# Column sums of the modulation vectors: two rows on two 32-column quarters of TensorE

## The chip, the cores and the metric

The kernel runs on one core of a Trainium2 chip. The core has a matrix engine (TensorE; in the profile PE for the matmuls and PEld for the weight loads), a vector engine (VectorE, DVE), a scalar engine (ScalarE, ACT), a general engine (GpSimd, POOL) and a queue engine (SyncE, SP), which in this kernel issues the DMAs. Matmuls read SBUF and write PSUM. The metric is the device time of one execution in microseconds.

## The reference

One step of a hybrid diffusion backbone with one layer: 128 context tokens and 2048 latent tokens, 1024 wide. What the change touches is the modulation: six vectors of 1024 for each of two conditionings (context and latent), from one matrix product.

```python
def modulation(cond, w_mod_l, b_mod_l):
    m = jax.nn.silu(cond) @ w_mod_l + b_mod_l
    return jnp.split(m[:, None, :], N_MOD, axis=-1)
...
def block(x, s0, mod, n_chunks, ...):
    sh1, sc1, ga1, sh2, sc2, ga2 = mod
    h = rmsnorm(x, norm_mix_l) * (1.0 + sc1) + sh1
    o, s_new = mixer(h, s0, n_chunks, ...)
    x = x + ga1 * o
    h = rmsnorm(x, norm_ffn_l) * (1.0 + sc2) + sh2
    x = x + ga2 * (jnp.square(jax.nn.relu(h @ w_ff1_l)) @ w_ff2_l)
    return x, s_new
```

The mixer holds two DeltaNet scans and a spatial gate between one input and one output projection.

## The kernel before

The kernel runs in stages. Up to about 400 us it normalises the tokens, projects them (`pj`, lines 220 to 222 with operands `kH`, `kL`, `wH`, `wL`), convolves (`cv`) and stores queries, keys and values. Then come the scans with the other projections and the output projection (to about 1238 us), and then the two FFN products, whose matmuls write the PSUM tile `f`. Nearly every matmul is one of three of `mm3` (lines 220 to 222): both operands are split into a high and a low part that are read as fp32r, and high x high, high x low and low x high are added up in PSUM. ScalarE makes the high parts and VectorE the low ones.

The 6144 columns of the modulation product are worked off in twelve chunks `jc` of 512. Chunks 0 to 3 come first, by plain matmuls (line 335). Chunk 4 is done by `split_mod_steps`. The other seven, 5 to 9 in the first stage and 10 and 11 in the first FFN product, are made by `mod_steps`. There a chunk's eight blocks of 128 x 512 weights are loaded one after the other (line 235), and VectorE multiplies each by a column of the activated conditioning `scond` and adds it up (lines 254 and 256) into two accumulators `acc`, one for each conditioning, of 128 partitions x 512. What is left is a sum over the 128 partitions, made by TensorE in `total()`: one fp32 matmul for each accumulator (line 270) with the weights `pick[:, c, :]`, two columns wide, of which column c holds ones and the other zeros. Both matmuls add into the same two PSUM partitions. VectorE then adds the bias row (line 274), which `bias` (line 265) has loaded onto two partitions, and a DMA stores both rows to `mod_d` in DRAM (line 275).

In the first stage the steps of a chunk are given out beside the feature tiles by `interleave`, and the row tile `mrow` has one buffer. In the FFN the steps are spread over the products from the middle on, the accumulators and the row are `macc` tiles, and `total` is a step of its own (`pair` is given there). The readers of `mod_d` are the column step `second_mods` (line 718, chunks 6 to 9), the rows of the first gate (line 213, chunks 4 and 5) and those of the second (line 1853, chunks 10 and 11).

What order the instructions of an engine have is settled when the program is built: the calls and their written-out times give a first order, and the tile framework places instructions by a simulated timeline (`_TC = dict(schedule_with_timeline_sim=True)`). All DMAs are issued by SP, in one order.

Of the kernel before, what the change touches and what calls it, by code (L numbers as in the profile page):

```python
# [8 lines left out]
F32 = mybir.dt.float32  # L9
# [5 lines left out]
ALU = mybir.AluOpType  # L15
# [3 lines left out]
P = 128  # L19
# [43 lines left out]
def hybrid_step(  # L63
# [7 lines left out]
    V, A, G, T = nc.vector, nc.scalar, nc.gpsimd, nc.tensor  # L71
    load = nc.sync.dma_start
    store = nc.sync.dma_start
# [18 lines left out]
    mod_d = dp.tile([2, 6 * D], F32, name="mod_d")  # L92
# [73 lines left out]
    smp = ctx.enter_context(tc.tile_pool(name="small", bufs=4, reuse_waits="tile"))  # L166
# [40 lines left out]
    def w512(name, dt=F32):  # L207
        return wp.tile([P, 512], dt, tag="w", name=name)
# [12 lines left out]
            T.matmul(ps, lh, rl, start=False, stop=False, skip_group_check=more)  # L221
            T.matmul(ps, ll, rh, start=False, stop=last and i == n - 1, skip_group_check=more)  # L222

    pick = smp.tile([P, 2, 2], F32, tag="pick", name="pick", bufs=1)
    V.memset(pick, 0.0)
    V.memset(pick[:, 0, 0:1], 1.0)
    V.memset(pick[:, 1, 1:2], 1.0)

    def mod_steps(jc, pool, stage=None, psum=None, pair=None):

        u = {}

        def fetch_raw(k):
            raw = stage() if stage else sp.tile([P, 512], F32, tag="raw", name="raw")
            load(out=raw, in_=w_mod[0, k * P : (k + 1) * P, jc * 512 : (jc + 1) * 512])
            return raw

        def f(k):
            if pair:
                if k == 0:  # L240
                    u[0], u[1] = fetch_raw(0), fetch_raw(1)
                raw = u.pop(k)
                if k + 2 < KT:
                    u[k + 2] = fetch_raw(k + 2)
            else:
                raw = fetch_raw(k)
            if k == 0:
                if pair:
                    u["acc"] = pair()
                else:  # L250
                    u["acc"] = [pool.tile([P, 512], F32, tag=f"acc{c}", name="acc", bufs=1) for c in range(2)]
            for c, acc in enumerate(u["acc"]):
                if k == 0:
                    V.tensor_scalar_mul(acc, raw, scond[:, k, c : c + 1])
                else:
                    V.scalar_tensor_tensor(out=acc, in0=raw, scalar=scond[:, k, c : c + 1], in1=acc,
                                           op0=ALU.mult, op1=ALU.add)
            if k == KT - 1 and not pair:
                total()
            elif k == KT - 1:  # L260
                u["row"] = pair()[0][0:2, :]
                bias(u["row"])

        def bias(row):
            load(out=row, in_=b_mod[0:1, jc * 512 : (jc + 1) * 512].to_broadcast([2, 512]))

        def total():
            ps = (psum or pm1)()
            for c, acc in enumerate(u["acc"]):
                T.matmul(ps[0:2, :], pick[:, c, :], acc, start=c == 0, stop=c == 1)  # L270
            row = u["row"] if pair else pool.tile([2, 512], F32, tag="mrow", name="mrow", bufs=1)
            if not pair:
                bias(row)
            V.tensor_tensor(out=row, in0=ps[0:2, :], in1=row, op=ALU.add)
            store(out=mod_d[:, jc * 512 : (jc + 1) * 512], in_=row)

        return [lambda k=k: f(k) for k in range(KT)] + ([total] if pair else [])

    head = {}

    with ExitStack() as ph:
# [8 lines left out]
        def pt():  # L290
            return ppt.tile([P, 512], F32, tag="pt", name="pt", bufs=3)
# [93 lines left out]
        ps = pt()  # L385
# [328 lines left out]
        def second_mods():  # L714
# [8 lines left out]
            for cd in range(2):  # L723
                V.scalar_tensor_tensor(out=a2[:, cd, :], in0=pc4[:, cd, 1, :], scalar=1.0, in1=vec[:, 24:32],
                                       op0=ALU.add, op1=ALU.mult)

        mods = [st for jc in range(4, 10) for st in (split_mod_steps(jc) if jc == 4 else mod_steps(jc, p1))]
        blk, xs_, cols = prep_block(0)
        for st in xs_:
# [30 lines left out]
        for bi in range(len(BLOCKS)):  # L760
# [8 lines left out]
            for n, (gi, h) in enumerate(order):  # L769
                u = us[n] if bi == 0 and n < 3 else feature_tile(blk, bi, gi, h)  # L770
# [156 lines left out]
    with ExitStack() as ph:  # L927
# [551 lines left out]
        for i, u in enumerate(units):  # L1479
# [3 lines left out]
            c = i % 2  # L1483
# [107 lines left out]
    def bank():  # L1591
        return psq.tile([P, 512], F32, tag="f", name="f", bufs=8)
# [19 lines left out]
    class Unit:  # L1612
# [6 lines left out]
        def load(self, i, kh):  # L1619
            for q in range(2):  # L1620
                self.raw[i, kh, q] = r = w512("raw")
                r0, c0 = kh * 512 + q * 256, self.jp * 512 + i * 256
                load(out=r.rearrange("p (a c) -> p a c", a=2),
                     in_=w_ff1[0, r0 : r0 + 256, c0 : c0 + 256].rearrange("(a p) c -> p a c", p=P))
# [130 lines left out]
    acc = {}  # L1755
# [210 lines left out]

    junk16 = smp.tile([P, 512], BF16, tag="junk16", name="junk16", bufs=1)
    mods = [st for jc in range(10, 12) for st in mod_steps(jc, wp, lambda: w512("mraw"), bank, mrow)]
    mods = {half + 28 + 4 * j: st for j, st in enumerate(mods)}

# [8 lines left out]
    for p, (o, n, m) in enumerate(seq):  # L1979
        u = units[n]  # L1980
# [37 lines left out]
    for m, (n, i, u, q) in enumerate(todo):  # L2018
# [6 lines left out]
        if q == 0:  # L2025
            ps = bank()
# [80 lines left out]
```

## Time and profile before

| what | us |
|---|---|
| median of 3 runs | 2574.07 |
| lowest and highest of the runs | 2570.79, 2575.09 |
| the profiled execution's own time | 2574.06 |
| its span in the profile | 2572.3 |
| PE busy | 2536.5 |
| PEld busy | 2132.5 |
| DVE busy | 1782.1 |
| ACT busy | 1192.8 |
| POOL busy | 315.1 |

The span is the time from the first to the last recorded instruction; the execution's own time has 1.8 us around it. The mean granted TensorE clock was 0.999. Busy times of different engines lie beside each other. A weight load usually lies beneath the matmul before it, so PEld and PE do not add up. A recorded matmul includes the end of its pipeline, so the pace is read from one start to the next. In a view of groups a row gives the line, the engine, the operation, the output and inputs and the count, then the least, median and greatest duration in ns and the first and last start in us. In a view of waits a row gives who waited, for whom, the total in us, the number of times and the longest.

### The profile page before, as it was taken

Reading aid. Unit: us, or ns where it says so; the run is one execution under the profiler, and the core shown is the slowest. Engines: PE = TensorE matmul, PEld = TensorE weight load, DVE = VectorE, ACT = ScalarE, POOL = GpSimd, SP = SyncE. Lnnn points to the kernel's source line nnn. Section 1 sums busy time; section 2 is a strip of 40 time slices with the busy share of each in tenths; the row PEclk is TensorE's granted clock in tenths of the full one; section 3 lists DMA queues with packets and bytes.
Section 4 is the critical chain, followed back from the end, with each engine's and each line's share of the span. In section 5 each row is a group of like instructions: output and inputs, shape, how many; then the busy total and the mean of one; then the engine's idle time right before and its main releaser. Section 6 shows DMA issues by size and latency. Waiting matters only on the chain.

```text
span 2572.3 us, 43717 instructions
## 1 busy us (share of the span) xinstructions
PE 2536.5 (99%) x15296; PEld 2132.5 (83%) x15296; DVE 1782.1 (69%) x3525; ACT 1192.8 (46%) x2758; POOL 315.1 (12%) x512
## 2 busy tenths in 40 slices
PE   8999999999999999999999999999999999999998
PEld 4999999788888788778888888888888888888887
DVE  5777746667667788885587886677674445684874
ACT  4755545554545566763355553333243333243441
POOL 3112112222222233331000000000000000000000
PEclk9999999999999999999999999999999999999999
DMA  8966637755556758896778788445599778686773
GB/s 285 299 225 205 191 126 219 246 161 171 171 169 179 228 185 270 279 304 209 274 219 249 221 289 279 140 147 152 180 299 323 267 258 296 241 259 211 232 253 105
DMA packets 533859, 579.77 MB, mean 225 GB/s; under 512 B 35500, under 2 KB 366684, under 8 KB 530054
## 3 DMA queue, kind: packets, MB, share of 16 engines
q1 hardware_dynamic: 533638, 576.98, 69.3%
q8 instruction: 120, 1.97, 0.3%
q14 instruction: 101, 0.83, 0.1%
HBM read 397.62 MB, written 179.22 MB: 224 GB/s over the span
## 4 chain that ended last, share of the span: by engine, by line
PE 55%; DVE 1%; issue 1%; DMA 0%; ACT 0%; POOL 0%; DVEq 0%; POOLq 0%; ACTq 0%
PE f L220 17%; PE f L221 17%; PE f L222 17%; PE pj L220 1%; PE pj L222 1%; PE pj L221 1%; PE f L856 0%; PE pd L994 0%; PE pd L1098 0%; PE pd L1099 0%; DMA hop_d<-opL 0%; PE pm L1415 0%; PE pd L1062 0%; PE f L270 0%; PE f L1738 0%
## 5 line engine op out<-in xcount | busy, mean ns | idle before, releaser
L220 PE MATMUL f<-hop,zH 128*128 128x512 f32 x960 | 373.2, 389 | 0.0
L222 PE MATMUL f<-hop,zL 128*128 128x512 f32 x960 | 373.1, 389 | 0.0
L221 PE MATMUL f<-hop,zH 128*128 128x512 f32 x960 | 373.1, 389 | 0.0
L220 PE MATMUL f<-hop,wH 128*128 128x512 f32 x896 | 351.4, 393 | 0.0
L221 PE MATMUL f<-hop,wH 128*128 128x512 f32 x896 | 348.9, 390 | 0.0
L222 PE MATMUL f<-hop,wL 128*128 128x512 f32 x896 | 344.3, 390 | 0.0
L1601 ACT CAST zH<-zraw 128x512 fp32r<-128x512 f32 x240 | 146.3, 620 | 286.1 <-DVE zraw L1595 87.4
L1595 DVE TENSOR_TENSOR zL<-zraw,zH 128x512 fp32r<-128x512 f32 x240 | 162.2, 687 | 77.6 <-ACT zH L1601 66.1
L221 PEld LDWEIGHTS f<-hop,zH 128*128 128x128 f32 x960 | 180.2, 188 | 37.4
L222 PEld LDWEIGHTS f<-hop,zL 128*128 128x128 f32 x960 | 180.2, 188 | 37.4
L220 PEld LDWEIGHTS f<-hop,zH 128*128 128x128 f32 x960 | 180.2, 188 | 37.3
L222 PEld LDWEIGHTS f<-hop,wL 128*128 128x128 f32 x896 | 168.2, 188 | 35.7
L220 PEld LDWEIGHTS f<-hop,wH 128*128 128x128 f32 x896 | 168.5, 188 | 33.9 <-issue 0.9
L221 PEld LDWEIGHTS f<-hop,wH 128*128 128x128 f32 x896 | 168.5, 188 | 32.2
L222 PE MATMUL pj<-kH,wL 128*128 128x386 f32 (+2 forms) x568 | 190.5, 335 | 0.0
L220 PE MATMUL pj<-kH,wH 128*128 128x386 f32 (+2 forms) x568 | 189.2, 336 | 0.5 <-DVE kH L487 0.3
L221 PE MATMUL pj<-kL,wH 128*128 128x386 f32 (+2 forms) x568 | 189.3, 333 | 0.0
L178 POOL TENSOR_TENSOR r<-rsq,nhalf 128x1 f32<-128x1 f32 (+1 forms) x38 | 23.0, 605 | 1351.8 <-DVE rsq L177 1351.8
L1748 ACT CAST wH<-s 128x512 fp32r<-128x512 f32 x96 | 58.9, 620 | 172.5 <-DVE s L1595 156.9
L537 DVE SCALAR_TENSOR_TENSOR cv<-pj,vec,cv 128x384 f32<-128x384 f32 (+2 forms) x164 | 87.1, 539 | 56.9 <-ACT cv L534 55.5
L220 PEld LDWEIGHTS pj<-kH,wH 128*128 128x128 f32 x568 | 107.1, 189 | 5.1 <-issue 4.7
L221 PEld LDWEIGHTS pj<-kL,wH 128*128 128x128 f32 x568 | 107.4, 189 | 0.5
(409 smaller groups left out, 5726.5 us busy)
## 6 DMA issues: line engine op xcount, KB each, us to landing
zraw<-z_d SPq DMA_DIRECT2D x212, 256.0 KB
raw<-in_w_ff_dram SPq DMA_DIRECT2D x128, 256.0 KB
hop<-hop_d SPq DMA_DIRECT2D x28, 1024.0 KB
z_d<-c SPq DMA_DIRECT2D x96, 256.0 KB
zraw<-s_d SPq DMA_DIRECT2D x96, 256.0 KB
raw<-in_w_mod_dram SPq DMA_DIRECT2D x80, 256.0 KB
r<-in_w_ff_dram SPq DMA_DIRECT2D x80, 256.0 KB
s_d<-s SPq DMA_DIRECT2D x64, 256.0 KB
```

The lines of the kernel that those rows point to most:

```text
L178: G.tensor_tensor(out=out, in0=t[:np_, :n], in1=nhalf[:np_, :n], op=ALU.pow)
L220: T.matmul(ps, lh, rh, start=first and i == 0, stop=False, skip_group_check=more)
L221: T.matmul(ps, lh, rl, start=False, stop=False, skip_group_check=more)
L222: T.matmul(ps, ll, rh, start=False, stop=last and i == n - 1, skip_group_check=more)
L537: V.scalar_tensor_tensor(out=cv[:, o : o + m], in0=ps[:, s + sh : s + sh + m], scalar=convw[:, w, j : j + 1], in1=cv[:, o : o + m], op0=AL ...
L1595: V.tensor_tensor(out=out, in0=a, in1=b, op=op)
L1601: A.copy(h, src)
L1748: A.copy(h, s2)
```

## The change

The two accumulators are no longer summed into two neighbouring partitions by matmuls of two columns each. `pick` is now one block of 32 columns with ones in the first and zeros in the others (a tile of 40 columns is allocated, of which 32 are used). Each accumulator has its own matmul, the first with its output on PSUM partitions 0 to 31, the second on 32 to 63, each started and stopped by itself. The sums stand on partitions 0 and 32. So the row tile reaches to partition 32, and the bias load, the add and the store are done once for each of the two rows.

```diff
-    pick = smp.tile([P, 2, 2], F32, tag="pick", name="pick", bufs=1)
+    pick = smp.tile([P, 40], F32, tag="pick", name="pick", bufs=1)[:, 0:32]
     V.memset(pick, 0.0)
-    V.memset(pick[:, 0, 0:1], 1.0)
-    V.memset(pick[:, 1, 1:2], 1.0)
+    V.memset(pick[:, 0:1], 1.0)
...
             elif k == KT - 1:
-                u["row"] = pair()[0][0:2, :]
+                u["row"] = pair()[0][0:33, :]
                 bias(u["row"])
 
+        def one(c):
+            return slice(32 * c, 32 * c + 1)
+
         def bias(row):
-            load(out=row, in_=b_mod[0:1, jc * 512 : (jc + 1) * 512].to_broadcast([2, 512]))
+            for c in range(2):
+                load(out=row[one(c), :], in_=b_mod[0:1, jc * 512 : (jc + 1) * 512])
 
         def total():
             ps = (psum or pm1)()
             for c, acc in enumerate(u["acc"]):
-                T.matmul(ps[0:2, :], pick[:, c, :], acc, start=c == 0, stop=c == 1)
-            row = u["row"] if pair else pool.tile([2, 512], F32, tag="mrow", name="mrow", bufs=1)
+                T.matmul(ps[32 * c : 32 * c + 32, :], pick, acc, start=True, stop=True)
+            row = u["row"] if pair else pool.tile([33, 512], F32, tag="mrow", name="mrow", bufs=1)
             if not pair:
                 bias(row)
-            V.tensor_tensor(out=row, in0=ps[0:2, :], in1=row, op=ALU.add)
-            store(out=mod_d[:, jc * 512 : (jc + 1) * 512], in_=row)
+            for c in range(2):
+                V.tensor_tensor(out=row[one(c), :], in0=ps[one(c), :], in1=row[one(c), :], op=ALU.add)
+                store(out=mod_d[c : c + 1, jc * 512 : (jc + 1) * 512], in_=row[one(c), :])
```

## The prediction, made before the change was run

> **What bounds the kernel now.** I began with the head of the profile page: which engine fills the span, and what the chain that ended last consists of.
>
> ```profile
> span 2572.3 us, 43717 instructions
> PE 2536.5 (99%) x15296; PEld 2132.5 (83%) x15296; DVE 1782.1 (69%) x3525; ACT 1192.8 (46%) x2758; POOL 315.1 (12%) x512
> PE 55%; DVE 1%; issue 1%; DMA 0%; ACT 0%; POOL 0%; DVEq 0%; POOLq 0%; ACTq 0%
> ```
>
> TensorE is busy for 99% of the span and is the only engine with weight in the chain; busy matmul time alone can mislead, because matmuls overlap. So I next read the busy time by stretches, in those parts where the change has its work (five of its seven places lie between 150 and 350 us, two between 1700 and 1850 us) and in what follows. The columns are the stretch, its length, and the busy time and count of PE, PEld, DVE, ACT and POOL.
>
> ```profile
> 150.00:200.00 50.00, 50.00 (x308) 47.58 (x307) 33.99 (x63) 25.75 (x73) 7.67 (x33) 1.00 0.73 242
> 300.00:350.00 50.00, 50.00 (x297) 45.83 (x296) 36.10 (x72) 26.98 (x80) 11.45 (x36) 1.00 0.57 179
> 400.00:650.00 250.00, 244.88 (x1990) 205.04 (x1989) 167.04 (x435) 127.59 (x312) 57.98 (x55) 1.00 0.66 206
> 650.00:900.00 250.00, 246.15 (x2192) 204.86 (x2188) 182.78 (x471) 132.34 (x289) 62.20 (x70) 1.00 0.60 185
> 900.00:1238.00 338.00, 329.87 (x2793) 274.60 (x2792) 265.95 (x581) 199.19 (x531) 98.38 (x87) 1.00 0.75 240
> 1700.00:1850.00 150.00, 150.00 (x735) 124.16 (x734) 104.03 (x165) 52.15 (x94) 0.00 (x0) 1.00 0.52 158
> ```
>
> The reader is to see that PE has no idle time at all where the changed matmuls stand (50.00 of 50, 150.00 of 150), at granted clock 1.00, and that DVE has 14 to 16 us free in every 50 there and 46 in the 150. PE is idle only between 400 and 1238 us: 5.12 + 3.85 + 8.13 = 17.1 us. Thus a microsecond of PE time saved at the seven places comes off the end, and work added to DVE or to the DMA queue there costs nothing until it makes PE wait.
>
> **The matmuls that change.** The rows of the tile `pick` come next, then the weight loads around one of the seven places.
>
> ```profile
> L270 PEld LDWEIGHTS pm<-acc,pick x20: 80/84/85, 153.8 to 348.7; 128*2 128x2 f32 x20
> L270 PE MATMUL pm<-acc,pick x20: 591/592/593, 153.8 to 349.1; 128*2 128x512 f32 x20
> L270 PE MATMUL f<-macc,pick x8: 591/592/592, 1719.0 to 1823.6; 128*2 128x512 f32 x8
> ```
>
> ```profile
> 153.38 0.34 PE L221 MATMUL pj<-kL,wH 128*128 128x386 f32 x1
> 153.56 0.33 PE L222 MATMUL pj<-kH,wL 128*128 128x386 f32 x1
> 153.83 1.88 PE L270 MATMUL pm<-acc,pick 128*2 128x512 f32 x4
> 155.64 0.44 PE L220 MATMUL pj<-kH,wH 128*128 128x386 f32 x1
> ```
>
> ```profile
> 153.83 0.09 PEld L270 LDWEIGHTS pm<-acc,pick 128*2 128x2 f32 x2 [0.25 <-issue]
> 154.26 0.08 PEld L270 LDWEIGHTS pm<-acc,pick 128*2 128x2 f32 x1 [0.35 <-issue]
> 154.69 0.09 PEld L270 LDWEIGHTS pm<-acc,pick 128*2 128x2 f32 x1 [0.34 <-issue]
> 155.63 0.19 PEld L220 LDWEIGHTS pj<-kH,wH 128*128 128x128 f32 x1 [0.86 <-issue]
> ```
>
> The counts are 20 and 8 where the source has two matmuls at each of 5 and 2 places: each fp32 matmul runs as two passes, with a weight load each, so one place has four passes (x4). The loads stand at 153.83 (two), 154.26 and 154.69; a load for the next pass goes out as the running pass begins, so a pass takes 154.26 - 153.83 = 154.69 - 154.26 = 0.43 us. The recorded 592 ns is longer than that because the ends overlap. From the first pass to the next ordinary matmul it is 155.64 - 153.83 = 1.81 us, which is 4 x 0.43 = 1.72 and 0.09 at the way out; at the way in, 153.83 - 153.56 = 0.27 against 0.18 for neighbours (153.56 - 153.38), another 0.09. The seven places together hold 7 x 4 x 0.43 = 12.0 us of passes, 0.47% of the span. That is all that can be won here.
>
> **The change part by part.** *Two column quarters.* Each row gets a matmul of its own (32 columns of weights, of which the first holds ones), the first into PSUM partitions 0 to 31, the second into 32 to 63. The number of passes stays four. What can change is that passes on different columns of the array run side by side. Passes go out in program order: first row pass 1, first row pass 2, second row pass 1, second row pass 2. Pass 2 of a row needs the same columns as its pass 1 and cannot start beside it; pass 1 of the second row can start right behind pass 2 of the first. That makes three slots of 0.43 in place of four: pass 1, then two together, then the last. No row of this trace shows two column parts in use at once, so the gain is bounded from both sides: no overlap gives 0, both rows wholly side by side saves two slots, 0.86 a place or 6.0 us. I take one slot, 7 x 0.43 = 3.0 us, because the row of loads shows that passes start in order and that a load is the only thing that goes out ahead.
>
> *Wider weights.* The row for a load of 128 columns is this:
>
> ```profile
> L221 PEld LDWEIGHTS f<-hop,zH 128*128 128x128 f32 x960 | 180.2, 188 | 37.4
> ```
>
> A load of 2 columns takes 84 ns and one of 128 columns 188 ns, so one of 32 columns should take about 84 + 30 x 104 / 126 = 109 ns, 25 more.
>
> Loads go out beneath the pass before, except the first of a place: 7 x 0.025 = +0.2 us. Bounds: 0 if the way in hides it, and +0.7 us if 25 ns are paid on all four loads (28 x 0.025). I take 0.2. The ways in and out (0.09 each) remain, since the matmuls of 2 columns already stand apart from full ones.
>
> Here a rule speaks against the change. The loads at 154.26 and 154.69 go out while a pass with all 128 rows is running. The Trainium skill, "TensorE: Matmul & The Clock Gate", section "Part 3: Packing small matmuls — row/col tiling", says that a weight load overlaps a running matmul only where the row groups differ; two column quarters share all four row groups, and by that rule the second row's load would wait and no slot be won. This trace disagrees for loads into the same columns; no row shows it for other columns.
>
> *Two adds and two bias loads in place of one.* The add on two partitions and the two DMAs are these:
>
> ```profile
> L274 DVE TENSOR_TENSOR mrow<-pm,mrow x5: 669/673/679, 156.5 to 349.7; 2x512 f32<-2x512 f32 x5
> L275 SPq DMA_DIRECT2D mod_d<-mrow x5: 248/253/319, 157.2 to 350.4; - x5
> L265 SPq DMA_DIRECT2D mrow<-in_b_mod_dram x5: 261/262/273, 127.3 to 306.6; - x5
> ...
> L1595 DVE TENSOR_TENSOR acc<-f,acc x18: 678/692/692, 2194.0 to 2481.1; 128x512 f32<-128x512 f32 x18
> ...
> DVE cv L537 <- ACT cv L534: 50.9, 27, 5.2
> SPq L275 <- DVE mrow L274: 6.2, 4, 2.4
> SPq L265 <- DMA mod_d<-mrow: 2.1, 3, 1.3
> PE pj L220 <- DVE cv L537: 0.2, 1, 0.2
> PE pj L609 <- DVE cv L537: 0.2, 1, 0.2
> ...
> ACT junk L435 <- DMA x<-in_x_sample_dram: 17.7, 6, 5.4
> ```
>
> The add of 2 partitions takes 0.67 us and one of 128 partitions 0.69, so one partition should cost as much as two: seven more adds, 7 x 0.67 = 4.7 us of DVE time. DVE spends 50.9 us between 120 and 415 us waiting for ACT's `cv`, so the 3.4 us that fall there fit in; PE waits for DVE 0.4 us in all of that time (the two PE rows). If that cover were gone each add would put `cv` or a weight split 0.67 us later, 4.7 us at most; I take 0. The queue gets 14 more DMAs: 7 x (0.25 + 0.26) = 3.6 us of issue. Behind the waiting instructions on SP stand the raw loads for later modulation steps, the stores of `kH`, `kL` and the features, and the x loads. SP already stands 6.2 us before its stores for the add and 2.1 us before the next bias load for the store (`mrow` has one buffer); each second store waits 0.67 more, and the next bias load for two stores. Who waits for what SP brings is ACT at the x loads (17.7 us in that time), not PE. Cost 0; bound, as above, the whole 3.6. The other reader is the column step at L718:
>
> ```profile
> L718 SPq DMA_DIRECT2D mrow<-mod_d x1: 767/767/767, 351.6 to 351.6; - x1
> L720 PE MATMUL pt<-ident,mrow x1: 243/243/243, 414.9 to 414.9; 32*128 32x32 f32 x1
> ...
> L1853 SPq DMA_DIRECT2D row<-mod_d x4: 320/320/320, 2369.4 to 2458.1; - x4
> L275 SPq DMA_DIRECT2D mod_d<-macc x2: 249/252/254, 1721.6 to 1825.5; - x2
> ```
>
> It loads at 351.6 and its transpose runs at 414.9, 63 us later; a second store behind it by under 2 us changes nothing. What the last two places write by 1825.5 us is read from 2369.4 us on.
>
> *The ones.* The memsets of `pick` look like this:
>
> ```profile
> L226 DVE MEMSET pick<- x1: 59/59/59, 1.7 to 1.7; 128x1 f32 x1
> ```
>
> Three of them become two; they end at 1.7 us, 152 us ahead of their first reader. I take 0. `pick` takes 160 bytes a partition in place of 16, so tiles placed behind it move.
>
> ```profile
> L222 PE MATMUL f<-hop,zL 128*128 128x512 f32 x960 | 373.1, 389 | 0.0
> L220 PE MATMUL f<-hop,wH 128*128 128x512 f32 x896 | 351.4, 393 | 0.0
> ```
>
> The FFN matmuls read operands from dozens of buffers, and the means of their groups lie between 389 and 393 ns. So I take 0 for the places; one nanosecond on each of these 5568 matmuls, either way, would be 5.6 us.
>
> **The sum.** -3.0 + 0.2 = -2.8 us against the profiled execution's 2574.06 us, which is 0.01 us from the median of the three runs (2574.07): **2571.2 us**, 0.11% less.
>
> **The rivals.** *No overlap* (the change doesn't do what it says): the second quarter's load or pass waits for the first. For it: nothing in the trace has ever run side by side. Against it: loads do go out ahead. Time: 2574.06 + 0.2 to 0.7, say 2574.5.
> *Both rows wholly side by side*: passes of the two rows pair up, two slots a place. For it speaks only that they share nothing but the order; against it, the order. Time: 2574.06 - 6.0 + 0.2 = 2568.2. The Trainium skill, in the section named above, gives packed matmuls a span of one matmul and about 4 ns for each further part, which amounts to this case; no row here shows it.
> *Slower, a new order*. Two of the longest waits of PE are these:
>
> ```profile
> PE pd L1189 <- DVE P L1178: 4.8, 10, 1.4
> PE pj L1415 <- DVE o L1400: 3.8, 3, 1.3
> ```
>
> The program is ordered at build time by a simulated timeline (`schedule_with_timeline_sim=True`). Longer adds and more DMAs there can shift what stands where between 400 and 1238 us, where PE already idles 17.1 us, about half of it at these two handovers. If that idle time grew by half, 8.5 us, the time would be 2574.06 - 2.8 + 8.5 = 2579.8. It makes the kernel slower than before from 2.8 us of growth on. Against it: the edits lie outside this stretch, 50 us before it or 480 after it, and between 350 and 400 us PE is full again.
>
> **How the numbers follow.** About 0.2% (5.1 us: below 2568.9, above 2579.2) is what a measurement of this kernel can tell from no change; the three runs span 0.17%. One slot saved 0.45; no overlap 0.28; two slots 0.15; a new order that costs 0.12. Faster by over 0.2% takes two slots, or one slot with a few us of luck from places or order: 0.15 + 0.05 = 0.20. Slower by over 0.2% is the last rival: 0.12. Within: 0.68. The range reaches down past two slots with the scatter of the runs, 2567.6, and up past no overlap with its bound and 2 us of scatter, 2577.2; it leaves out most of the last rival and the far tail of the second, under 0.2.
>
> **What would show it.** In the changed profile the loads of L270's successor at one place tell the slots: the first pass to the next ordinary matmul takes 1.38 us with three slots, 0.95 with two, 1.81 with four. PE should still have no idle time from 150 to 350 us; DVE should have 14 adds of about 0.67 us on one partition. The prediction is wrong if PE waits for DVE or DMA beside these places, if the idle time between 400 and 1238 us is far from 17.1 us, or if the ordinary matmuls have another pace than before.

## The result and the profile after

| what | us |
|---|---|
| before, median of 8 runs | 2573.71 (2570.79 to 2575.55) |
| changed kernel, median of 8 runs | 2580.74 (2578.67 to 2582.27) |
| ratio of changed to before | 1.0029, 95% interval 1.002 to 1.0038 |

The changed kernel is slower by 0.29%, some 7 us. The forecast was 2571.2 us, and 2577.2 at most.

The head of its page, to be read against the head shown before:

```profile
span 2580.5 us, 43754 instructions
PE 2545.6 (99%) x15296; PEld 2132.2 (83%) x15296; DVE 1789.1 (69%) x3531; ACT 1193.0 (46%) x2758; POOL 319.3 (12%) x512
PE 56%; DVE 1%; DMA 1%; issue 1%; ACT 0%; SPq 0%; POOL 0%; DVEq 0%; POOLq 0%; ACTq 0%
```

PE has the same 15296 matmuls and still fills the span, 9.1 us longer busy. The first question is whether the changed places got slower. These are the rows of `pick` in the changed kernel, and PE's instructions in order of time at the first place (start, length, engine and line, operation, output and inputs, shape):

```profile
L273 PEld LDWEIGHTS pm<-acc,pick x20: 106/108/110, 152.3 to 330.0; 128*32 128x32 f32 x20
L273 PE MATMUL pm<-acc,pick x20: 592/605/618, 152.3 to 330.4; 128*32 128x512 f32 x20
...
L273 PE MATMUL f<-macc,pick x8: 592/605/617, 1719.4 to 1822.8; 128*32 128x512 f32 x8
```

```profile
152.08 0.33 PE L222 MATMUL pj<-kH,wL 128*128 128x386 f32 x1
152.34 1.05 PE L273 MATMUL pm<-acc,pick 128*32 128x512 f32 x4
153.33 0.45 PE L220 MATMUL pj<-kH,wH 128*128 128x386 f32 x1
```

The four passes take 153.33 - 152.34 = 0.99 us where they took 1.81: not three slots but two. The places won more than was forecast, 0.82 us each.

One of the seven gave some of it back. Its two matmuls stand 10 us apart in the new order, at 320.02 and 329.97, and each has to itself the short extra time that the prediction calls the ways in and out:

```profile
320.02 1.04 PE L273 MATMUL pm<-acc,pick 128*32 128x512 f32 x2
321.00 0.45 PE L220 MATMUL pj<-kH,wH 128*128 128x386 f32 x1
```

So that place takes 2 x 0.98 = 1.96 us where it took 1.81, and a second way in of 0.09. Six places win 6 x 0.82 = 4.9 us and the seventh loses 0.15 + 0.09 = 0.24.

The time went elsewhere. These are the busy times by stretches (stretch, its length, then PE, PEld, DVE, ACT and POOL) for the part in which PE had idle time before:

```profile
400.00:650.00 250.00, 245.47 (x1992) 204.96 (x1990) 166.21 (x433) 128.28 (x312) 57.87 (x55) 1.00 0.66 208
650.00:900.00 250.00, 245.53 (x2180) 204.50 (x2180) 183.59 (x471) 128.61 (x280) 61.79 (x70) 1.00 0.59 185
900.00:1238.00 338.00, 329.68 (x2782) 274.26 (x2781) 265.38 (x578) 199.15 (x532) 98.31 (x87) 1.00 0.74 239
```

PE is idle there for 4.53 + 4.47 + 8.32 = 17.3 us, against 17.1 before: the recurrence did not get worse. What did is the ordinary matmul. The groups of the second FFN product in the changed kernel have a mean of 392 ns where they had 389:

```profile
L222 PE MATMUL f<-hop,zL 128*128 128x512 f32 x960 | 375.8, 392 | 0.0
L220 PE MATMUL f<-hop,zH 128*128 128x512 f32 x960 | 375.7, 392 | 0.0
L221 PE MATMUL f<-hop,zH 128*128 128x512 f32 x960 | 375.6, 392 | 0.0
```

A recorded length includes the pipeline's end, so the pace is better read from starts. Here are a stretch of the kernel before, and then the same one of the changed kernel:

```profile
2000.02 0.39 PE L220 MATMUL f<-hop,zH 128*128 128x512 f32 x1
2000.25 0.39 PE L221 MATMUL f<-hop,zH 128*128 128x512 f32 x1
2000.47 0.39 PE L222 MATMUL f<-hop,zL 128*128 128x512 f32 x1
2000.70 0.39 PE L220 MATMUL f<-hop,zH 128*128 128x512 f32 x1
...
2001.38 0.39 PE L220 MATMUL f<-hop,zH 128*128 128x512 f32 x1
```

```profile
2000.15 0.40 PE L220 MATMUL f<-hop,zH 128*128 128x512 f32 x1
2000.39 0.39 PE L221 MATMUL f<-hop,zH 128*128 128x512 f32 x1
2000.62 0.40 PE L222 MATMUL f<-hop,zL 128*128 128x512 f32 x1
2000.85 0.39 PE L220 MATMUL f<-hop,zH 128*128 128x512 f32 x1
...
2001.55 0.40 PE L220 MATMUL f<-hop,zH 128*128 128x512 f32 x1
```

Six matmuls take 2001.38 - 2000.02 = 1.36 us before and 2001.55 - 2000.15 = 1.40 after: 227 ns and 233 ns from start to start, at the same granted clock (1.00). No idle time shows, no wait, no other work of PE: the matmuls are 3% slower on average.

It is not every matmul. The `hop` tiles, the moving operand of these FFN matmuls (the one that streams past the loaded weights), lie in two pools: two at the right end of SBUF (`hopA`), five on the left behind `wp`, whose tiles hold the weights (`wH`, `wL`, `zH`, `zL`). The starts in the traces, put beside the addresses of the tiles in the built programs, part the 5450 FFN matmuls that another follows without a break (within 300 ns) like this (mean ns from a matmul's start to the next one's):

| hop tile | product | matmuls | before | changed |
|---|---|---|---|---|
| left | first | 1843 | 227.51 | 227.56 |
| left | second | 1653 | 226.68 | 227.25 |
| right | first | 730 | 227.79 | 232.79 |
| right | second | 1224 | 226.69 | 232.90 |

The means hide a pattern: from the third matmul of a right-hand stretch on, the starts in the changed kernel's second product are 237 and 229 ns apart by turns.

The loss is 730 x 5.0 = 3.7 us, 1224 x 6.2 = 7.6 and 1653 x 0.57 = 0.9: 12.2 us in all. What sets the right-hand tiles apart is the distance from the other operand; so far this is argued, and the experiments test it. `pick` grew from 32 bytes (16, padded) to 160, so `wp` and all that lies on the left moved up by 128 bytes (`wp` from 13696 to 13824) while `hopA`, which hangs at the right end, stayed at 196480. Before, left and right had the same remainder modulo 512; now they differ by 128. Left-hand hop tiles moved with `wp`, and between them nothing changed.

The sum comes out: -4.9 + 0.24 + 12.2 = +7.5 us, where the medians differ by 2580.74 - 2573.71 = 7.0 and the two profiled executions by 2582.27 - 2574.06 = 8.2.

### The profile page after: what moved, and what is told of

Same layout as the page of the kernel before. It is cut to its first block, busy times and chain, and to the rows that moved or that the text cites. A ratio compares the mean times of both kernels' runs of the same rounds, so it can differ in the third digit from the quotient of the medians.

```text
span 2580.5 us, 43754 instructions
## 1 busy us (share of the span) xinstructions
PE 2545.6 (99%) x15296; PEld 2132.2 (83%) x15296; DVE 1789.1 (69%) x3531; ACT 1193.0 (46%) x2758; POOL 319.3 (12%) x512
## 4 chain that ended last, share of the span: by engine, by line
PE 56%; DVE 1%; DMA 1%; issue 1%; ACT 0%; SPq 0%; POOL 0%; DVEq 0%; POOLq 0%; ACTq 0%
PE f L220 17%; PE f L221 17%; PE f L222 17%; PE pj L220 1%; PE pj L222 1%; PE pj L221 1%; PE f L860 0%; PE pd L998 0%; PE pd L1102 0%; PE pd L1103 0%; DMA gr<-g_d 0%; DMA hop_d<-opL 0%; PE pm L1419 0%; DMA ob<-ob_d 0%; PE pd L1066 0%
```

## The experiments

Theory D: the distance between the operands, by its remainder, sets the pace of the ordinary matmuls. Rival Q: the 32-column quarters leave the array slower for what follows. Rival A: the new place of the left-hand operands counts, by itself. "The small tile at the right end" is `zcol`, of which a third is used.

### The move without the change

The kernel before, with a wider tile for `pick` and nothing else:

```diff
-    pick = smp.tile([P, 2, 2], F32, tag="pick", name="pick", bufs=1)
+    pick = smp.tile([P, 40], F32, tag="pick", name="pick", bufs=1)[:, 0:4].rearrange("p (c a) -> p c a", c=2)
```

> The kernel before with only the tile of pick grown from 16 to 160 bytes; matmuls, adds and DMAs as before. Theory D (distance: the FFN matmuls lose time because the left side of SBUF, where the split operands lie, moves by 128 bytes against the hop tiles fixed to the right end): the FFN matmuls on the right-hand hop tiles go from 226.7 to about 233 ns from start to start, 1954 of them, so about 12 us slower than before, 2585 to 2587 us. Rival Q (the 32-column quarters themselves leave the array slower): as before, 2573.7.

Measured: 2586.51 us against 2573.07 (21 runs of before), ratio 1.0057, interval 1.0044 to 1.007. Its matmuls on right-hand tiles start every 232.8 and 232.9 ns (first and second product). In its built program the matmuls of the seven places stand at the same points of PE's order as in the kernel before, so these 13 us are the move's alone; Q falls as the cause.

### The change without the move

The changed kernel with a column of ones that is read 32 times:

```diff
-    pick = smp.tile([P, 40], F32, tag="pick", name="pick", bufs=1)[:, 0:32]
-    V.memset(pick, 0.0)
-    V.memset(pick[:, 0:1], 1.0)
+    pick = smp.tile([P, 4], F32, tag="pick", name="pick", bufs=1)[:, 0:1]
+    V.memset(pick, 1.0)
+    pick = pick.to_broadcast([P, 32])
```

> The changed kernel with pick in 16 bytes again: a column of ones read 32 times (step 0) as weights, so every output row of a quarter holds the sum. No tile behind it moves. D: ordinary FFN matmuls back to 226.7 ns, the seven places at 0.98 us each, so 2573.7 - 4.8 = 2569 us. Q: as the changed kernel, 2580.7.

Measured: 2569.74 us against 2573.07, ratio 0.9989, interval 0.998 to 0.9998. The groups of the second product are back:

```profile
L220 PE MATMUL f<-hop,zH 128*128 128x512 f32 x960 | 373.2, 389 | 0.0
L222 PE MATMUL f<-hop,zL 128*128 128x512 f32 x960 | 373.1, 389 | 0.0
L221 PE MATMUL f<-hop,zH 128*128 128x512 f32 x960 | 373.1, 389 | 0.0
```

The places are those of the changed kernel (0.98 us, one still apart). So the quarters with the second adds, loads and stores do make the kernel faster, by 3 us between the medians and 4.3 between the profiled executions (2574.06 and 2569.74).

### The distance made from the other side

The kernel before, with the right-hand tiles moved down by 128 bytes:

```diff
-    zcol = edge.tile([P, 3 * KT], F32, name="zcol")[:, 0:KT]
+    zcol = edge.tile([P, 7 * KT], F32, name="zcol")[:, 0:KT]
```

> The kernel before with the small tile at the right end of SBUF grown by 128 bytes, so the hop tiles at the right move down by 128 and nothing on the left moves. D: same distance as in the changed kernel, modulo 512, so about 11 to 12 us slower than before, 2585 to 2586. Rival A (it is the moved place of the left-hand operands by itself): as before, 2573.7.

Measured: 2586.99 us against 2573.07, ratio 1.0051, interval 1.0038 to 1.0063. Nothing on the left moved, and the right-hand matmuls start every 232.8 and 232.9 ns. A falls.

### Every place moved, the distance kept

The kernel of the second experiment with `pick` allotted 24 columns and `zcol` 8 in place of 24:

```diff
-    zcol = edge.tile([P, 3 * KT], F32, name="zcol")[:, 0:KT]
+    zcol = edge.tile([P, KT], F32, name="zcol")[:, 0:KT]
...
-    pick = smp.tile([P, 4], F32, tag="pick", name="pick", bufs=1)[:, 0:1]
+    pick = smp.tile([P, 24], F32, tag="pick", name="pick", bufs=1)[:, 0:1]
```

> The changed kernel's matmuls with left-hand tiles moved up by 64 bytes and the right-hand hop tiles up by 64 as well, so the distance is as before and every place is another. D: 2569 us, ordinary FFN matmuls at 226.7 ns. A: slower than that, 2573 us or more, ordinary FFN matmuls over 229 ns.

Measured: 2570.83 us against 2573.07, ratio 0.9988, interval 0.9979 to 0.9997; right-hand matmuls at 227.7 and 226.7 ns. Both sides moved by 64, and the pace is the old one. It is the distance.

That other engines get in PE's way at the wrong distance is a rival that the traces can test. In the second product of the changed kernel 281 right-hand matmuls have no recorded VectorE, ScalarE or GpSimd instruction beside them (from 230 ns before their start to 230 ns after it). They start every 233.0 ns, and the other 943 every 232.9. DMAs can't be set aside in this way, since they run all through the product.

### Which distances

The same kernel with three more distances, made by the widths of the two tiles (24 columns for `pick`, 72 for `pick`, 8 for `zcol`):

> The changed kernel's matmuls, left-hand tiles 64 bytes higher than before, right-hand hop tiles in place (distance 64). 128 was slow, so no modulus that divides 128 can be the rule. If only the remainder modulo 512 or 256 counts: ordinary matmuls on the right-hand hop tiles slower than 226.7 ns. If the loss grows with the distance, about half of the 6 ns of distance 128: 230 ns, 2575 us; if any other remainder costs the same: 233 ns, 2581 us.

> The same with a distance of 256. If the modulus is 256: 226.7 ns and 2569.7 us. If it is 512: slower, 233 ns and 2581 us or more (it is the farthest from a whole multiple).

> The same with the right-hand hop tiles 64 bytes higher and the left-hand tiles where they were before: distance 448, or -64. If the loss depends on the size of the distance alone, as the run with distance 64; if on its sign too, another pace, between 226.7 and 235 ns.

| distance modulo 512 | right, first product, ns | right, second product, ns | median us | ratio to before, interval |
|---|---|---|---|---|
| 0 | 227.80 | 226.69 | 2569.74 | 0.9989, 0.998 to 0.9998 |
| 64 | 233.54 | 233.34 | 2582.48 | 1.0036, 1.0025 to 1.0048 |
| 128 (the change) | 232.79 | 232.90 | 2580.74 | 1.0029, 1.002 to 1.0038 |
| 256 | 227.80 | 226.69 | 2569.54 | 0.9983, 0.9972 to 0.9994 |
| 448 | 231.25 | 229.79 | 2577.89 | 1.0018, 1.0007 to 1.003 |

256 costs no more than 0, so the remainder modulo 512 is not what counts; all five fit a remainder modulo 256. That the cost of 64 or 128 comes back at 320 or 384 was not tried. The loss neither grows with the distance (64 costs no less than 128) nor is it the same for 64 and -64 (448). At 448 the lines are no longer alike either:

```profile
L220 PE MATMUL f<-hop,zH 128*128 128x512 f32 x960 | 377.2, 393 | 0.0
L222 PE MATMUL f<-hop,zL 128*128 128x512 f32 x960 | 375.7, 392 | 0.0
L221 PE MATMUL f<-hop,zH 128*128 128x512 f32 x960 | 373.6, 389 | 0.0
```

Line 221 keeps 389 ns while 220 has 393. The two multiples of 256 are free and the three distances between multiples are not; what form the loss has there stays open. The version with 256 is faster than both kernels; against the changed one it has 72 columns allotted to `pick` in place of 40, and reads one column of ones 32 times.

### Which pass goes first

The kernel of the second experiment, with 16 weight columns for the second row, so that its passes bear another shape:

```diff
             for c, acc in enumerate(u["acc"]):
-                T.matmul(ps[32 * c : 32 * c + 32, :], pick, acc, start=True, stop=True)
+                n = 16 if c else 32
+                T.matmul(ps[32 * c : 32 * c + n, :], pick[:, 0:n], acc, start=True, stop=True)
```

> The changed kernel with pick in 16 bytes and the second row's matmul on 16 weight columns in place of 32, so that the two rows' passes can be told apart in the profile (128x32 and 128x16). The program lists first row pass 1, pass 2, then second row pass 1, pass 2. If the chip lets the second row's passes overtake: starts of 32, 16, then 32, 16 columns, two slots of 0.43 us. If both passes of a row can run at once: 32, 32, then 16, 16. Time as with 32 columns, 2569.7 us.

One run, 2568.09 us. The groups by shape in the first 0.09 us of the first place (153.21 to 153.30 us; columns as in the view of groups):

```profile
L274 PE MATMUL pm<-acc,pick 128*32 128x512 f32 x1 | 0.6, 616 | 0.0
L274 PE MATMUL pm<-acc,pick 128*16 128x512 f32 x1 | 0.6, 602 | 0.0
```

One pass of each row has begun, the first row's first and the second row's 7 ns behind it, and the other two follow some 0.45 us later, again one of each (the second row's first). In the compiled program both passes of the first row stand ahead of both of the second. So the second row's passes overtake the first row's second pass: the order that is settled when the program is built is not in every case the order in which TensorE starts its passes. That the pass overtaken waits for its own columns fits this, but is not shown apart. The Trainium skill, "TensorE: Matmul & The Clock Gate", section "Part 3: Packing small matmuls — row/col tiling", says that matmuls begin and end strictly in program order; these runs show otherwise. For packed matmuls it gives a span of one matmul and some 4 ns for each further part, where these runs show 7 ns from the first part's start to the second's.

## Why the prediction was wrong

- **Bound.** Right. PE fills the span in both kernels, and what PE won or lost came out at the end.
- **Two column quarters.** The direction was right, the size too small: I took one slot a place, 3.0 us in all, and two were saved. The step that failed is "Passes go out in program order". It rested on the order of loads in a trace in which all passes used the same columns, and it left the rival that came true (both rows side by side) only 0.15. With it right the sum would have been 2568.2, and the error larger still.
- **Wider weights.** The length was right, 106 to 110 ns a load where 109 was worked out. The 0.2 us for it did not show: all four loads are out within 0.04 us at the head of a place, and at the first one the way in takes 152.34 - 152.08 = 0.26 us, where it took 0.27. What the prediction cites from the Trainium skill, "TensorE: Matmul & The Clock Gate", section "Part 3: Packing small matmuls — row/col tiling", that a load overlaps a running matmul only where the row groups differ, is contradicted: the second row's load goes out 5 ns after the first pass begins.
- **Two adds and DMAs.** Right. The adds on one partition take 0.68 us, DVE is busy 204.85 us between 120 and 415 us where it was 199.72, and SP stands 12.0 us before the stores for the add, up from 6.2. PE hardly notices: its waits there come to 0.7 + 0.3 + 0.2 = 1.2 us, against 0.4. These are the rows of the changed kernel, first of the tile, then of the waits between 120 and 415 us:

```profile
L278 DVE TENSOR_TENSOR mrow<-pm,mrow x10: 667/680/684, 154.5 to 331.8; 1x512 f32<-1x512 f32 x10
```

```profile
SPq L279 <- DVE mrow L278: 12.0, 7, 5.5
...
PE pt L593 <- ACT ev L596: 0.7, 2, 0.5
PE pj L613 <- DVE cv L541: 0.3, 1, 0.3
PE pj L220 <- DVE cv L541: 0.2, 1, 0.2
```

- **The places. This is the step that made the forecast wrong.** I wrote "So I take 0 for the places", because groups whose operands lie in dozens of buffers had nearly one mean, and put a nanosecond a matmul at 5.6 us without carrying that into the range. The evidence could not show what it was used for: every one of those buffers, left or right, has the same remainder modulo 256, since all are 2048 or 16384 bytes long and the two ends had been brought into step by the unused part of `zcol`. Many places were seen, but one distance only. Two distances are now known: the right-hand matmuls lose 5.0 to 6.2 ns each, and the term that was put at 0 is 12 us. Another pace of the ordinary matmuls is among the signs of being wrong that the prediction names, and it is the one that came.
- **The rivals.** No overlap: no. Slower by a new order: no; the idle time between 400 and 1238 us is 17.3 us where 17.1 were, and the one thing that the new order cost is the pair that stands apart, 0.24 us and the 0.82 that it did not win. The slower side was right for a reason that none of the rivals held.

## What to carry to other kernels

A tile that changes its size moves all that is allocated behind it on its side of SBUF, and not what hangs at the other end. In a kernel whose matmuls fill the time, compare the distance between the operands of its main loop before and after, by its remainder modulo 256 (0 was the free one here), ahead of any count of instructions. And where a trace shows one value for all places, ask first whether the places differ in what might matter; to hold a move at nothing takes a trace with two distances in it.

## What was not expected of the hardware

- The right-hand fp32r matmuls of the second FFN product (128 x 512) start every 226.7 ns when the distance between the two operands is 0 or 256 bytes, and every 229.8 to 233.3 ns at the other distances tried, with no wait, gap or clock in the profile that tells it. The Trainium skill, "SBUF — State Buffer", section "Who interferes with whom", says that PE never waits on anyone in SBUF; here two reads of PE itself are the likeliest reading, though no run shows the reads themselves. Which two is open: the weights of the running matmul and those loaded beneath it have one remainder in all these kernels, so they were not told apart.
- The matmuls of the first stage, with a moving operand of 386 columns, occur in the kernel before at both distances, 0 and 128 modulo 256, and start every 175 to 180 ns (medians by line) at either. There the distance shows no cost; why was not tried.
- In the second product, matmuls on left-hand tiles lose 0.6 ns when the right-hand ones are 128 off (226.68 to 227.25), though their own distance is unchanged. In the trace of the changed kernel nearly all of this lies in the first three matmuls behind a right-hand tile, which take 231.5, 232.6 and 230.7 ns on average; from the fourth on they are back at 226.7. Why the loss outlasts the tile is open.
- Two fp32 matmuls on different quarters take the time of one: four passes in 0.98 us, and 0.98 us for each matmul of the pair that stands apart. Their passes do not keep the program's order.
